# Rank scatter: 14 of 128 tiles as direct row copies, five scatters split into 2 and 126 rows

## The chip, the cores and the metric

One core of a Trainium2 chip. The metric is the device time of one execution in microseconds; lower is better. The core has a matrix engine (PE), a vector engine (DVE), GpSimd (POOL), ScalarE (ACT), SyncE (SP), and 16 DMA engines that all transfers share. SP and ACT issue plain transfers, POOL issues the indirect ones.

## The reference

Eight batches of 2048 rows, each row 2560 floats (10,240 bytes). Each row goes to the place that its score has among the 2048 scores of its batch.

```python
B, N, D = 8, 2048, 2560           # x: (B, N, D), scores: (B, N)
order = np.argsort(scores, axis=1)
ranks = np.argsort(order, axis=1)
out = np.zeros_like(x)
out[np.arange(B)[:, None], ranks, :] = x
```

x and out have 167.8 MB each; a rank is the number of scores in the batch that are smaller (plus the equal ones that stand earlier).

## The kernel before

The rows are cut into 128 tiles (b, t) of 128 rows: eight batches b, sixteen tiles t in each. All waits are placed by hand: each engine has a counter (`Line`), and `after` makes one engine wait for another's count.

- **Ranks.** The scores (64 KB) are loaded once, turned on PE into `s_col` (a score per partition), and for each batch spread over all partitions into `s_all` (PE into `ps_all`, DVE copies it, L206). For each tile DVE then counts with three reductions (L225) how many scores are smaller, adds the three counts (L248, L254) into `rank`, and turns it into whole numbers in `rank_i` (L265). DVE works through the tiles in order and never waits for the rows.
- **Loads.** `load` (L294) brings tile k of 128 rows, 1.28 MB of `x`, into buffer k % 16. The loads alternate between SP (even k) and ACT (odd k). The first sixteen go out at once; a later one first waits (`scatter_done`) until the scatter of the tile that had its buffer, sixteen before, has landed.
- **Scatters.** POOL goes through the tiles in order (`scatter`, L345). For each it waits for the load and for DVE's ranks, and issues an indirect DMA that writes the 128 rows of the buffer to the 128 rows of `out` that `rank_i` names.
- **The lists.** `DIRECT[b]` names the tiles of batch b that are not loaded and scattered but copied by rows, and `SPLIT` the tiles whose scatter is issued in two pieces: the last `LAST` = 2 rows with their own copy of the ranks (`rank_t`, on the first partitions), and the other 126. `BULK` is the list of the tiles that are loaded, `ROWS` of those that are copied. In the kernel before, both lists are empty, so all 128 tiles are in `BULK` and the code for rows and pieces makes no instructions.
- **Order on SP and ACT.** The lists of the two queues are written out in one loop over k, from NBUF = 16 on: ahead of load k all groups of rows come that are due by then, alternately on SP and ACT:

```python
for k in range(NBUF, NB):
    while n < len(chunks) * (k - NBUF + 6) // (NB - NBUF + 6 + 6):
        rows(*two[n % 2], *chunks[n])
        n += 1
    load(two[k % 2][0], k)
```

A group (`chunks`) has G = 16 rows, so a tile copied by rows has eight groups.

Of the kernel before, what the change touches and what calls it, by code (L numbers as in the profile page):

```python
# [40 lines left out]
def kernel(  # L41
# [7 lines left out]
    B, N, D = x.shape  # L49
# [3 lines left out]
    T = N // P  # L53


    DIRECT = [()] * B

    SPLIT = ()
    LAST = 2
    ORDER = [list(range(T)) for b in range(B)]  # L60
    BULK = [(b, t) for b in range(B) for t in ORDER[b] if t not in DIRECT[b]]
    ROWS = [(b, t) for b in range(B) for t in DIRECT[b]]
    NB = len(BULK)
# [28 lines left out]
    with tc.tile_critical(no_gpsimd_drain=True):  # L92
# [86 lines left out]
        def from_psum():  # L179
            b, t, tick = pending  # L180
            dve.after(pe, tick)
            col = b * T + t
            if t in DIRECT[b]:
                t_rows[b, t] = dve.did(
# [16 lines left out]
        for b in range(B):  # L201
# [12 lines left out]
            for t in ORDER[b]:  # L214
# [43 lines left out]
                if pending is not None:  # L258
                    from_psum()
                    pending = None  # L260
                direct = t in DIRECT[b]
                if not direct:
# [4 lines left out]
                if direct:  # L267
# [5 lines left out]
                    ))  # L273
                elif (b, t) in SPLIT:
                    pe.after(dve, dve.n)
# [22 lines left out]
        def scatter_done(line, k):  # L298
            line.wait(s_scat[k % NBUF], 16 * (k // NBUF + 1))
            n = sum(1 for j in range(k % NBUF, k + 1, NBUF) if BULK[j] in SPLIT)  # L300
            if n:
# [40 lines left out]
        def scatter(k, lo, hi, index, sem):  # L342
            b, t = BULK[k]
            col = b * T + t
            nc.gpsimd.indirect_dma_start(  # L345
                out=out_flat,
                out_offset=bass.IndirectOffsetOnAxis(
                    ap=index[:hi - lo, col:col + 1], axis=0
                ),
                in_=xb[k % NBUF][lo:hi, :],  # L350
                in_offset=None,
                element_offset=b * N * D,
            ).then_inc(sem, 16)

        for k, (b, t) in enumerate(BULK):
            i = k % NBUF
            pl.wait(s_load[i], 16 * (k // NBUF + 1))
            pl.after(dve, t_bulk[b, t])
            if (b, t) in SPLIT:
                scatter(k, P - LAST, P, rank_t, s_last[i])  # L360
# [33 lines left out]
```

## Time and profile before

| | |
|---|---|
| median of 3 runs | 798.27 us (798.03 to 798.38) |
| profiled execution | 798.03 us |
| its span in the profile | 796.3 us |
| instructions in the profile | 1925 |
| busy: PE, DVE, POOL | 29.3, 422.3, 122.6 us |
| read from and written to HBM | 167.84 MB and 167.77 MB |
| 128 scatters: issue on POOL, median from issue to landing | 949 ns each, 87.4 us |
| 64 loads on SP: median from issue to landing | 10.3 us |

The span is cut into 40 equal slices in the profile, each digit the busy share of a slice in tenths. For the DMA engines the digit is the mean over the 16, and a line of GB/s says what they moved; a transfer is counted once, whether it goes in or out. A queue's share is the time that its packets took, as a share of 16 engines over the span. In a wait, "SPq" is SP's queue of DMA issues; behind the arrow stands what it waited for, then the time in all, how often, and the longest. In a table by windows each line has the window, its length, the busy time of PE, PE's weight loads, DVE and POOL with the number of instructions, the granted PE clock, the DMA share and the GB/s. In the timeline a line has the start and the time from the first to the last of the instructions merged in it, which "x6" counts.

### The profile page before, as it was taken

To read this page: it belongs to the slowest core of one execution; us is meant where nothing else is said; L and a number is where in the kernel's file an instruction comes from. 1 tells how busy PE (TensorE), PEld (TensorE's weight loads), DVE (VectorE), ACT (ScalarE), POOL (GpSimd) and SP (SyncE) were. 2 spreads that over 40 slices of the span, in tenths; PEclk is the share of its full clock that TensorE was granted. 3 is DMA by queue.
4 is the path that set the end of the run, shared out by engine and by line. 5 is a ranking of instruction groups with operands and counts; after the bars stand their busy time and mean duration, and the time that the engine had idled before them with its cause. 6 is when DMAs were issued, how large, how long until landed. Compare 5 with 4: busy or idle time off the path is not lost.

```text
span 796.3 us, 1925 instructions
## 1 busy us (share of the span) xinstructions
PE 29.3 (4%) x144; PEld 26.4 (3%) x144; DVE 422.3 (53%) x1170; POOL 122.6 (15%) x136
## 2 busy tenths in 40 slices
PE   3001001010010010010000000000000000000000
PEld 3001001010010010010000000000000000000000
DVE  6999999999999999999999200000000000000000
POOL 1211121111111111111111111111111111111100
PEclk9555555555555555555555555555555555555555
DMA  9999999999999999999999999999999999999995
GB/s 360 423 429 427 428 429 429 428 429 427 429 427 429 428 430 429 430 428 428 428 428 428 430 430 430 428 429 429 428 428 430 430 430 429 428 429 428 428 430 219
DMA packets 36893, 335.74 MB, mean 422 GB/s; under 512 B 4104, under 2 KB 4104, under 8 KB 4104
## 3 DMA queue, kind: packets, MB, share of 16 engines
q0 software_dynamic: 18432, 167.78, 49.7%
q10 hardware_dynamic: 9216, 83.89, 24.9%
q1 hardware_dynamic: 9232, 83.96, 24.9%
q14 instruction: 12, 0.10, 0.0%
q8 instruction: 1, 0.02, 0.0%
HBM read 167.84 MB, written 167.77 MB: 421 GB/s over the span
## 4 chain that ended last, share of the span: by engine, by line
another core or an unknown queue 81%; DMA 7%; DVE 3%; ACTq 2%; PE 1%; issue 0%; POOL 0%; SPq 0%; POOLq 0%
DMA out_dram<-x,rank_i 6%; ACTq L294 2%; DVE trash L225 2%; DMA x<-in_x_dram 1%; PE ps_all L161 0%; DMA s_in<-in_scores_dram 0%; PE ps_col L140 0%; DVE rank L254 0%; DVE rank L248 0%; POOL out_dram L345 0%; DVE rank_i L265 0%; DVE s_all L206 0%; DVE s_col L148 0%; SPq L389 0%
## 5 line engine op out<-in xcount | busy, mean ns | idle before, releaser
L225 DVE TENSOR_SCALAR_CACHE_REDUCE trash<-s_all,s_col 128x256 bf16<-128x256 f32 (+15 forms) x248 | 315.1, 1307 | 0.3
L345 POOL DMA_INDIRECT out_dram<-x,rank_i x128 | 121.5, 949 | 626.7 <-DMA x<-in_x_dram 435.6
L225 DVE SCALAR_TENSOR_TENSOR trash<-s_all,s_col,mask 128x128 bf16<-128x128 f32 x128 | 44.5, 347 | 0.0
L161 PE MATMUL ps_all<-ident,s_col 128*128 128x128 f32 x128 | 27.4, 403 | 307.8 <-DVE s_all L206 307.4
L161 PEld LDWEIGHTS ps_all<-ident,s_col 128*128 128x128 f32 x128 | 24.6, 215 | 310.3 <-DVE s_all L206 309.8
L254 DVE TENSOR_TENSOR rank<-rank,acc 128x1 f32<-128x1 f32 x128 | 20.5, 160 | 4.4
L248 DVE TENSOR_TENSOR rank<-acc,acc 128x1 f32<-128x1 f32 x128 | 20.4, 159 | 4.4
L265 DVE CAST rank_i<-rank 128x1 int32<-128x1 f32 x128 | 19.7, 154 | 4.5
L206 DVE COPY s_all<-ps_all 128x512 f32<-128x512 f32 x32 | 20.2, 684 | 2.2 <-PE ps_all L161 1.6
L225 DVE DVE_READ_ACCUMULATOR trash<-s_all,s_col 128x1 f32 x248 | 20.5, 83 | 0.0
L225 DVE DVE_READ_ACCUMULATOR trash<-s_all,s_col,mask 128x1 f32 x128 | 10.5, 82 | 0.0
L148 DVE COPY s_col<-ps_col 128x128 f32<-128x128 f32 x1 | 0.3, 292 | 4.6 <-PE ps_col L140 4.6
L140 PE MATMUL ps_col<-ident,s_in 8*128 8x8 f32 x16 | 1.9, 250 | 4.0 <-DMA s_in<-in_scores_dram 4.0
L140 PEld LDWEIGHTS ps_col<-ident,s_in 8*128 8x128 f32 x16 | 1.8, 216 | 4.0 <-DMA s_in<-in_scores_dram 4.0
L135 DVE MEMSET acc<- 128x128 f32 x1 | 0.2, 165 | 1.1 <-SPq L92 1.1
L111 POOL TENSOR_SCALAR_AFFINE_SELECT ident<-ident 128x128 f32<-128x128 f32 x1 | 0.3, 283 | 0.1
L123 POOL TENSOR_SCALAR_AFFINE_SELECT mask<-mask 128x128 f32<-128x128 f32 x1 | 0.3, 283 | 0.0
L107 POOL MEMSET ident<- 128x128 f32 x1 | 0.2, 204 | 0.5 <-SPq L92 0.5
L108 POOL MEMSET mask<- 128x128 f32 x1 | 0.2, 202 | 0.0
L378 POOL MEMSET const-float32-0.0<- 128x1 f32 x1 | 0.1, 99 | 0.3 <-issue 0.3
L378 POOL MEMSET const-uint8-127<- 128x1 uint8 x1 | 0.1, 120 | 0.0
L378 POOL MEMSET const-bfloat16-1.0<- 128x1 bf16 x1 | 0.1, 114 | 0.0
(1 smaller groups left out, 0.1 us busy)
## 6 DMA issues: line engine op xcount, KB each, us to landing
x<-in_x_dram ACTq DMA_DIRECT2D x64, 1280.0 KB
x<-in_x_dram SPq DMA_DIRECT2D x64, 1280.0 KB, 10.3
out_dram<-x,rank_i POOLq DMA_INDIRECT x128, 87.4
s_in<-in_scores_dram SPq DMA_DIRECT2D x1, 64.0 KB
```

The costliest lines, as they stand in the source:

```text
L111: nc.gpsimd.affine_select(out=ident[:], in_=ident[:], pattern=[[-1, P]], compare_op=OP.not_equal, fill=1.0, base=0, channel_multiplier=1,)
L123: nc.gpsimd.affine_select(out=mask[:], in_=mask[:], pattern=[[-1, P]], compare_op=OP.is_ge, fill=0.0, base=-1, channel_multiplier=1,)
L140: nc.tensor.transpose(out=ps_col[:, B * c:B * (c + 1)], in_=s_in[:, P * c:P * (c + 1)], identity=ident[:B, :B],)
L161: nc.tensor.transpose(out=ps_all[:, P * c:P * (c + 1)], in_=s_col[:, c, b:b + 1].to_broadcast([P, P]), identity=ident[:],)
L206: nc.vector.tensor_copy(out=s_all[:, 512 * q:512 * (q + 1)], in_=ps_all[:, 512 * q:512 * (q + 1)],)
L225: how.pop("do")(out=trash[i][:, :P * (hi_t - lo_t)], in0=s_all[:, P * lo_t:P * hi_t], accum_out=acc[which][:, cols], **how,)
L248: nc.vector.tensor_tensor(out=rank[:, cols], in0=acc[0][:, cols], in1=acc[1][:, cols], op=OP.add)
L254: nc.vector.tensor_tensor(out=rank[:, cols], in0=rank[:, cols], in1=acc[2][:, cols], op=OP.add)
L265: nc.vector.tensor_copy(out=rank_i[:, cols], in_=rank[:, cols])
L294: line.eng.dma_start(out=xb[i][:], in_=x[b, P * t:P * (t + 1), :]).then_inc(s_load[i], 16)
L345: nc.gpsimd.indirect_dma_start(out=out_flat, out_offset=bass.IndirectOffsetOnAxis(ap=index[:hi - lo, col:col + 1], axis=0), in_=xb[k % NBU ...
L378: nc = _bacc.Bacc("TRN2", target_bir_lowering=False, num_devices=1)
```

## The change

```diff
-    DIRECT = [()] * B
-
-    SPLIT = ()
+    DIRECT = [(4, 5)] * 6 + [(4,)] * 2
+
+    SPLIT = [(b, 8) for b in range(2, 7)]
```

- **Rows.** Tiles 4 and 5 of batches 0 to 5 and tile 4 of batches 6 and 7, fourteen tiles of 1792 rows, leave `BULK`, which has 114 tiles then. For each of them PE turns the ranks into one row (`ps_row`, L270), and DVE makes byte offsets of them (`rows_i`, L185) in place of the cast at L265, after the two additions of the next tile. Each of the 112 groups waits for that tile's offsets, loads 16 of them into registers of SP or ACT (L306), and issues 16 DMAs (L316). Each of these copies one row of 10,240 bytes from `x` to `out`, without a buffer; in the built program it is an access of 16 pieces of 640 bytes.
- **Their place.** With NB = 114 six groups stand ahead of load 16, three on each queue; from there on about one group comes with each load, and eight groups, four on each queue, follow after the last load. At the end SP and ACT also wait for all rows.
- **Pieces.** The scatter of tile 8 in batches 2 to 6 becomes two indirect DMAs on POOL, rows 126 and 127 first, then rows 0 to 125. PE picks out the two ranks (L277) and DVE copies them to `rank_t` (L196) after the additions of the next tile. A load into that buffer waits for both.
- The counting on DVE, the sixteen buffers and the order of the other tiles stay as they are. POOL has 119 indirect DMAs in place of 128, SP 954 DMAs in place of 65, ACT 953 in place of 64.

## The prediction

> **What bounds the kernel now.** I read the page first: the forty slices, then the DMA queues.
>
> ```profile
> PE   3001001010010010010000000000000000000000
> ...
> DVE  6999999999999999999999200000000000000000
> POOL 1211121111111111111111111111111111111100
> ...
> DMA  9999999999999999999999999999999999999995
> GB/s 360 423 429 427 428 429 429 428 429 427 429 427 429 428 430 429 430 428 428 428 428 428 430 430 430 428 429 429 428 428 430 430 430 429 428 429 428 428 430 219
> ```
>
> The 16 DMA engines are busy from the first slice to the last but one at a constant 429 GB/s; DVE, which counts the ranks, is done past the middle and POOL is nearly idle. The rate does not change when DVE stops, so DVE does not set it.
>
> ```profile
> DMA packets 36893, 335.74 MB, mean 422 GB/s; under 512 B 4104, under 2 KB 4104, under 8 KB 4104
> ...
> q0 software_dynamic: 18432, 167.78, 49.7%
> q10 hardware_dynamic: 9216, 83.89, 24.9%
> q1 hardware_dynamic: 9232, 83.96, 24.9%
> q14 instruction: 12, 0.10, 0.0%
> ```
>
> Each tile passes the engines twice: as a load (q1 for SP, q10 for ACT) and as a scatter (q0). The three shares add to 99.5%. All small packets are semaphore increments. Then the waits of the queues, and of the scatters:
>
> ```profile
> SPq L294 <- DMA out_dram<-x,rank_i: 708.0, 56, 24.3
> ```
> ```profile
> POOL out_dram L345 <- DMA x<-in_x_dram: 435.6, 84, 7.0
> ```
>
> SP waits 708 us for scatters to free buffers; POOL waits mostly for loads. The ring load, scatter, buffer is held up by the engines alone, with some fourteen scatters in backlog (87.4 us from issue to landing, at 6.1 us a tile). Last the end, by windows:
>
> ```profile
> 100.00:780.00 680.00, 18.27 (x80) 16.38 (x80) 332.54 (x926) 102.30 (x108) 0.51 1.01 429
> ...
> 785.00:786.00 1.00, 0.00 (x0) 0.00 (x0) 0.00 (x0) 0.00 (x0) 0.50 0.87 369
> 786.00:787.00 1.00, 0.00 (x0) 0.00 (x0) 0.00 (x0) 0.00 (x0) 0.50 0.22 92
> 787.00:789.00 2.00, 0.00 (x0) 0.00 (x0) 0.00 (x0) 0.00 (x0) 0.50 0.12 51
> 789.00:792.40 3.40, 0.00 (x0) 0.00 (x0) 0.00 (x0) 0.00 (x0) 0.50 0.06 24
> 792.40:796.30 3.90, 0.00 (x0) 0.00 (x0) 0.00 (x0) 0.00 (x0) 0.50 0.01 2
> ```
>
> 429 GB/s over 16 is 26.8 GB/s an engine. So most engines end at 786.0 us, and from 789 to 792.4 the 24 GB/s are one engine alone, 6.4 us late. After that 3.9 us of ending follow.
>
> **The price of a row now.** A 10,240-byte row takes 10240/26.8 = 382 ns of one engine per pass, its share of semaphore packets included. A tile is 8 load rows and 8 scatter rows per engine, 16 x 0.382 = 6.11 us, which the spacing of SP's loads confirms (12.2 us for two tiles). Per row of a tile: 6.11/128 = 47.7 ns of every engine.
>
> **The change, part by part.** *Fourteen tiles as row copies.* 1,792 rows go from x to out directly. Each is one DMA of 16 pieces of 640 bytes, one piece and one semaphore increment per engine. Each byte passes the engines once, not twice, but in small pieces. The trace has no 640-byte packet and no copy between two DRAM tensors. From below: 640/10240 x 382 = 24 ns of data, plus 6 ns for the increment (in the packet records of the tail, 387 ns from row to row with an increment between and 381 without), 30 ns. From above: an increment or 32-byte packet lasts 7 to 9 ns, nearly all fixed cost; 24 + 7 + 9 = 40 ns. Farther above: each byte billed for its reading and for its writing, as in a load and a store, 2 x 24 + 7 + 9 = 64 ns. The far ends: a first packet of the scores' load, with nothing pipelined ahead, took 773 ns on average for 8 KB against 307 ns in a full pipe; I leave those 466 ns out because other queues keep the pipe full here. I take 24 + 7 + 6 = 37 ns, near the additive bound, as fixed costs are what the small packets show. Gain per row 47.7 - 37 = 10.7 ns; times 1,792, 19.2 us off every engine. Without fixed cost it is 31.7 us; at 47.7 ns nothing.
>
> The Trainium skill speaks against taking the pure byte price: "DMA: Bandwidth & Descriptors", section "How a descriptor splits into AXI transactions", lets a piece that starts off a 256-byte boundary fetch wasted beats, so of 640-byte pieces every second one takes 24 beats for 20; with the 3 beats per packet of "Why small descriptors are slow" and 1.2 ns a beat (385 ns for 320) I estimate 33 ns with the increment on one half of the engines, 38 on the other, and the dearer half would make the gain 17 us. No run here shows it yet.
>
> *Issuing them.* SP and ACT each gain 896 row DMAs and 56 register loads, ahead of and between their loads. The price of an issue:
>
> ```profile
> 2.34 3.54 SPq L294 DMA_DIRECT2D x<-in_x_dram  x6
> ```
> ```profile
> 30.22 0.33 SPq L294 DMA_DIRECT2D x<-in_x_dram  x1
> ```
>
> 0.33 us alone, 0.59 us when both queues issue back to back. I take 0.59, as both will issue in runs of 16. A register load of 16 offsets has no row; bounds are nothing and a few issues (2 us); I take 1 us. One load and one group of 16 rows on a queue: 0.33 + 1 + 16 x 0.59 = 10.8 us. The engines need, for the two queues' two tiles and 32 rows, 2 x 6.11 + 32 x 0.037 = 13.4 us. So issue hides under the engines, with 2.6 us spare; it stops hiding at (13.4 - 1.33)/16 = 0.75 us a row.
>
> *What stands behind the rows.* The 17th and 18th loads, the first on each queue to reuse a buffer, now wait behind three groups each. Their offsets exist when DVE has finished tile 5, near 30 us, so the 17th load goes from 30.2 us to about 30 + 3 x 10.4 = 61 us. By then POOL will have issued some eleven scatters (one per 3.2 us from 14.8, less the two row tiles): with 16 loads 27 passes, 27 x 3.05 = 82 us of engine work. The engines don't run dry; the cover is 21 us and is gone at 1.0 us a row. Later a freed buffer waits up to one group, about 10 us of the backlog's 87. Four groups per queue come after the last load: 42 us against 53 us that now pass from ACT's last load at 738.9 to the last scatter's landing. Hidden.
>
> *Split scatters.* Five tiles go as 2 and 126 rows: five more POOL starts, against fourteen fewer; at 0.95 us each and 627 us of POOL idle, nothing. On DVE fourteen casts (154 ns) go, nineteen small copies out of PSUM come, the nearest 292 ns: about 3 us more, beside a DVE that has ended 340 us early. The scatters that wait for them (on tile 8 of batches 2 to 6) are by then late for loads. PE's 19 small operations lie in 308 us of idle. On the engines: 126 rows do not divide by 16. If 14 engines carry 9 rows each, they pay one row more per split, 5 x 0.382 = 1.9 us; the engines of the 2 rows carry one instead of eight and save 5 x 7 x 0.382 = 13.4 us. An even deal would cost 0. I take 1.9. (The Trainium skill, same page, section "Why a DMA increments its semaphore by 16 and not by 1", says that the largest divisor up to 16 is used, 14 for 126; the scores' load of 8 rows left 16 packets above 9,216, 8 data and 8 increments, which agrees.)
>
> *The late engine.* 6.4 us may be the instruction fetches (q14), if one engine does them; some 2,000 more instructions at 12 packets of about 0.33 us per 1,925 add 4 us. If the splits relieve this very engine (10.4 - 13.4 - 1.9 is below zero) it is no longer last; if they miss it, it is 10.4 us late. The trace doesn't say which; between the ends I take 3.2 us, nearer to relief.
>
> **Sum.** Engines 786.0 - 19.2 + 1.9 = 768.7; late engine 3.2; ending 3.9: a span of 775.8 us. The profiled execution took 798.03 us at a span of 796.3, 1.7 more, and lies 0.24 below the median; so 777.5, which I round to 777.
>
> **Rivals.**
> *Issue-bound (slower).* Rows with a register address issue slower than the 0.59 us seen for loads, or a row's ring turn behind 382 ns packets of the other queues sets the pace. The queue then lasts 30 + 56 x (16t + 1) + 57 x 0.33: past 768.7 from t = 0.74 us. At 0.85 it is 867 us, and 872 with the ending. For it: 0.82 us is the longest SP load issue at the start. Against: alone it is 0.33. Chance 0.12.
> *Copies between DRAM tensors cost both sides (slower).* At 64 ns a row the engines gain 29 us: 786.0 + 29.2 + 1.9 + 3.2 + 3.9 + 1.7 = 826. It is slower from about 50 ns, where 1,792 x 2.3 eats what the late engine gives. Against: a load and a scatter both cost 382 ns a row, so the end of the transfer hasn't mattered. Chance 0.07.
> *Dear but under break-even:* 42 to 48 ns or a late engine missed, 790 to 796. Chance 0.08.
> *Cheap:* 30 ns and a relieved engine: 786.0 - 31.7 + 0 + 3.9 + 1.7 = 760. Chance 0.08.
> *The sides cancel,* within 0.2% (1.6 us, about what a measurement of this kernel can tell from no change): 0.03.
> *Forecast,* 761 to 790: 0.62.
>
> **The numbers.** The range 761 to 796 holds the forecast, the dear case, half of the cheap and the cancelled one: about 0.77; widening it to the slower rivals at 826 and 872 would cover a gap that no case fills. Faster 0.62 + 0.08 + 0.08 = 0.78; same 0.03; slower 0.19.
>
> **What would show it.** Bytes fall by 14 x 1.31 = 18 MB to about 317, with 28,672 packets of 640 bytes and as many more increments. The engines' share stays at nine tenths in all slices and the rate falls to about 410 GB/s. SP still waits hundreds of us for scatters. The tail below full rate shrinks from 6.4 us. Slices below nine tenths, an SP that waits for no scatter, or rows issued at 0.75 us or more would prove the issue rival; full engines with a longer span, the second.

## The result and the profile after

The changed kernel takes 948.93 us (median of 4, 948.25 to 951.51) against 798.33 us: 1.189 times as long, 95% interval 1.187 to 1.192. The forecast was 777 us with a range to 796. The side was wrong: of the rivals, "issue-bound (slower)" was the right one in kind, with 872 us at the row price of 0.85 us that it took as its example.

The page of the changed kernel, the slices and the DMA queues:

```profile
span 946.5 us, 5641 instructions
...
DMA  9999999999999999899998899899999989999841
GB/s 367 424 427 416 357 382 359 343 374 335 365 327 371 329 371 322 297 353 319 381 302 308 313 341 365 313 337 342 350 344 327 319 307 377 350 359 360 314 162 20
DMA packets 90474, 317.74 MB, mean 336 GB/s; under 512 B 32568, under 2 KB 61240, under 8 KB 61240
...
q0 software_dynamic: 16656, 149.43, 39.2%
q10 hardware_dynamic: 36880, 83.95, 28.6%
q1 hardware_dynamic: 36896, 84.01, 25.5%
q14 instruction: 41, 0.34, 0.1%
```

The bytes fall to 317.74 MB as forecast. The rate was to fall to about 410 GB/s. It is 416 to 427 in slices 2 to 4, until 95 us, and from slice 5 on it swings between 297 and 382, until the list of rows runs out in the last two. The digits stay at 8 or 9 until then: the records count time in which a packet moves less than it could (between 100 and 870 us a 10,240-byte packet on ACT's queue takes 497 ns on average, against 385 in the kernel before), so a busy share near one with fewer bytes than 429 GB/s is no proof of work. Who waits for whom, SP first, then POOL:

```profile
SPq L306 <- DVE trash L225: 26.4, 2, 25.5
...
SPq L92 <- DMA out_dram<-in_x_dram: 6.3, 1, 6.3
```
```profile
POOL out_dram L345 <- DMA x<-in_x_dram: 652.0, 46, 40.5
```

SP waited 708 us for scatters before, and doesn't wait for one now. That and slices below nine tenths are two of the signs that the prediction had named for the issue rival. Buffers are free; the loads come late, and POOL waits 652 us for them, up to 40.5 us at a time. The timeline of SP's queue in the middle shows why: one load, sixteen rows, one load, without a pause.

```profile
427.88 14.16 SPq L316 DMA_DIRECT2D out_dram<-in_x_dram  x16
442.10 0.71 SPq L294 DMA_DIRECT2D x<-in_x_dram  x1
443.92 13.42 SPq L316 DMA_DIRECT2D out_dram<-in_x_dram  x16
457.39 1.17 SPq L294 DMA_DIRECT2D x<-in_x_dram  x1
459.68 14.67 SPq L316 DMA_DIRECT2D out_dram<-in_x_dram  x16
474.44 0.59 SPq L294 DMA_DIRECT2D x<-in_x_dram  x1
```

Load to load is 16 us, where the sum had 10.8 for the list and 13.4 for the engines. By line and operation (durations least, median, greatest):

```profile
L316 SPq DMA_DIRECT2D out_dram<-in_x_dram x896: 3/557/3152, 31.6 to 931.2; - x180
```
```profile
L306 SPq TENSOR_LOAD <-rows_i x56: 967/1159/2937, 29.9 to 920.3; - x56
```

The median row is issued in 557 ns, near the 0.59 us assumed, but the tail reaches 3.2 us. Added up over SP's records, from each start to the next: rows 725.6 us (0.81 each, the third sign), moves of their addresses 58.6, register loads 79.0, loads 66.9, of which 25 are the first wait for ranks. These 930 us are nearly all of the span. The list of SP, and ACT's like it, is the bound. Why a row whose issue needs 0.56 us takes 0.81 is what the experiments had to find.

### The profile page after: what moved, and what is told of

Its sections match the earlier page's. It is cut to its first block, busy times and chain, and to the rows that moved or that the text cites. A ratio compares the mean times of both kernels' runs of the same rounds, so it can differ in the third digit from the quotient of the medians.

```text
span 946.5 us, 5641 instructions
## 1 busy us (share of the span) xinstructions
PE 35.0 (4%) x168; PEld 27.7 (3%) x168; DVE 422.1 (45%) x1175; POOL 114.3 (12%) x127
## 2 busy tenths in 40 slices
DMA packets 90474, 317.74 MB, mean 336 GB/s; under 512 B 32568, under 2 KB 61240, under 8 KB 61240
## 3 DMA queue, kind: packets, MB, share of 16 engines
q10 hardware_dynamic: 36880, 83.95, 28.6%
## 4 chain that ended last, share of the span: by engine, by line
issue 48%; DVE 43%; POOL 5%; PE 1%; DMA 0%; POOLq 0%; SPq 0%
DVE trash L225 35%; POOL out_dram L345 5%; DVE rank L248 2%; DVE rank L254 2%; DVE s_all L206 2%; DVE rank_i L265 2%; PE ps_all L161 0%; DMA s_in<-in_scores_dram 0%; DVE rows_i L185 0%; PE ps_col L140 0%; POOLq L28 0%; DVE s_col L148 0%; DVE rank_t L196 0%; SPq L389 0%; SPq L92 0%
## 5 line engine op out<-in xcount | busy, mean ns | idle before, releaser
L345 POOL DMA_INDIRECT out_dram<-x,rank_i x114 | 108.8, 955 | 740.4 <-DMA x<-in_x_dram 596.4
L265 DVE CAST rank_i<-rank 128x1 int32<-128x1 f32 x114 | 17.3, 152 | 3.5
L345 POOL DMA_INDIRECT out_dram<-x,rank_t x5 | 4.3, 865 | 56.0 <-DMA x<-in_x_dram 55.7
L270 PE MATMUL ps_row<-ident,rank 128*1 128x128 f32 x14 | 5.2, 372 | 147.2 <-DVE rank L254 117.6
L225 DVE DVE_READ_ACCUMULATOR trash<-s_all,s_col,mask 128x1 f32 x128 | 10.3, 81 | 0.0
L270 PEld LDWEIGHTS ps_row<-ident,rank 128*1 128x1 f32 x14 | 1.1, 79 | 151.3 <-DVE rank L254 119.5
L185 DVE TENSOR_SCALAR rows_i<-ps_row 1x128 int32<-1x128 f32 x14 | 3.8, 272 | 0.0
L277 PE MATMUL ps_last<-rank,ident 128*2 128x1 f32 x10 | 1.0, 164 | 50.3 <-DVE rank_i L265 50.3
L277 PEld LDWEIGHTS ps_last<-rank,ident 128*2 128x2 f32 x10 | 0.4, 82 | 51.8 <-DVE rank_i L265 51.8
L196 DVE CAST rank_t<-ps_last 2x1 int32<-2x1 f32 x5 | 0.7, 139 | 0.0
## 6 DMA issues: line engine op xcount, KB each, us to landing
out_dram<-x,rank_i POOLq DMA_INDIRECT x114, 14.8
```

What stands on the lines that cost most here:

```text
L185: nc.vector.tensor_scalar(out=rows_i[ROWS.index((b, t))][:], in0=ps_row[:1, :P], scalar1=float(b * N), scalar2=float(ROW), op0=OP.add, op1 ...
L196: nc.vector.tensor_copy(out=rank_t[:, col:col + 1], in_=ps_last[:LAST, col:col + 1])
L225: how.pop("do")(out=trash[i][:, :P * (hi_t - lo_t)], in0=s_all[:, P * lo_t:P * hi_t], accum_out=acc[which][:, cols], **how,)
L265: nc.vector.tensor_copy(out=rank_i[:, cols], in_=rank[:, cols])
L270: nc.tensor.transpose(out=ps_row[:1, :P], in_=rank[:, cols], identity=ident[:])
L277: nc.tensor.matmul(out=ps_last[:LAST, cols], lhsT=ident[:, P - LAST:], rhs=rank[:, cols], start=True, stop=True,)
```

## The experiments

Each ratio is against runs of the kernel before on the same chip, with its 95% interval. Unless said otherwise `SPLIT = ()`.

**First, parts of the change.** Rows without splits:

```diff
-    SPLIT = [(b, 8) for b in range(2, 7)]
+    SPLIT = ()
```


> The fourteen row tiles, no split scatters. Issue theory (the lists of SP and ACT are the bound: about 30 us, then 56 groups of 16 rows at 0.875 us a row and 1.4 us for the register load, then the loads): 949 us, unchanged within 0.5%, since POOL and the late DMA engine are not on the path. If the split scatters cost the time (126 rows on few engines): much faster, below 850 us.

942.86 us, ratio 1.181 (1.179 to 1.183), a little below the 949 us within 0.5%. The rows alone make the loss; the splits add 6 us to it.

Splits without rows:

```diff
-    DIRECT = [(4, 5)] * 6 + [(4,)] * 2
+    DIRECT = [()] * B
```


> No row tiles, five scatters split. If a split relieves the engine that ends 6.4 us late before: 798.3 - 6.4 + 1.9 = about 794 us. If it relieves other engines: 798.3 + 1.9 = about 800 us. If 126 rows fall on one engine: over 900 us.

808.36 us (803.8 to 813.5), ratio 1.014 (1.011 to 1.017). Worse than either way of relief on the list and far from the 900 us, so none of the three cases, and with more spread than most kernels here. From 790 to 796 us its windows still show 97 to 148 GB/s, the work of four to six engines after the others have ended, where before it was one.

Half the rows:

```diff
-    DIRECT = [(4, 5)] * 6 + [(4,)] * 2
+    DIRECT = [(4,)] * 7 + [()]
```


> Seven row tiles (896 rows), no splits: half the row DMAs. Issue theory: a queue's list lasts about 30 + 28 x 15.4 + 60 x 0.65 = 500 us, under the engines' time, so the engines bind again and the bytes saved show: 798.3 - 896 x (47.7 - 39 ns) = about 790 us, with SP waiting for scatters again for over 200 us. Engine theory (small packets slow the DMA engines themselves): half of the loss stays, about 873 us.

814.66 us, ratio 1.020 (1.019 to 1.022). Neither: far from half the loss, and still a loss. The issue of a row had grown, not shrunk. SP's timeline here:

```profile
496.34 28.58 SPq L316 DMA_DIRECT2D out_dram<-in_x_dram  x16
524.97 0.57 SPq L294 DMA_DIRECT2D x<-in_x_dram  x1
```

28.6 us for sixteen rows, 1.8 us each. The price of an issue isn't fixed: with fewer rows the DMA engines were busier (402 GB/s on average against 336) and the queue waited more for them. The median landing of SP's loads is 49.0 us, from 10.3 before: loads stand behind rows within the queue too.

Fewer bytes in each row:

```diff
-                    out=out_bytes[bass.ds(at[i], ROW)],
-                    in_=x_bytes[b, P * t + G * q + i, :],
+                    out=out_bytes[bass.ds(at[i], 1024)],
+                    in_=x_bytes[b, P * t + G * q + i, :1024],
```
(with the splits of the changed kernel)


> As the changed kernel, but each row DMA copies only the first 1,024 of the 10,240 bytes (16 pieces of 64 bytes); the rest of those rows is left out. Issue theory with a price of its own per DMA: 949 us within 3%. If the issue waits for the engines to take the bytes, or the engines are the bound: the engines lose 1,792 x 21 ns = 38 us of work each, and the time falls by 30 us or more, to 910 us or less.

The kernel leaves out nine tenths of each copied row. Four runs, 916 to 942 us: the spread is nearly as wide as the difference asked about, and the lowest lies between the two expectations. Against 949 us the bytes left out are worth 7 to 33 us of the 150; the runs say no more.

**Second, the price on the engines against the place in the queues.** My reading of the seven tiles was that a row costs the engines 66 ns, not 37. Two row tiles:

```diff
+    DIRECT = [(4,)] * 2 + [()] * 6
```


> Two row tiles (256 rows, in batches 0 and 1), no splits: so few that neither list of SP or ACT is near its limit. Dear-copy theory (from seven tiles: (814.66 - 798.46)/896 = 18 ns a row lost net, so 66 ns of every engine): 798.5 + 256 x 18 ns = 803 us. The 37 ns on record: 798.5 - 256 x 10.7 ns = 796 us. Pure issue theory (the copies are cheap, the lists are the bound): also 796 us.

796.42 us, ratio 0.9973 (0.9963 to 0.9983): a gain. (798.49 - 796.42)/256 = 8 ns a row, against 10.7 in the prediction. The 66 ns fell.

Rows on ACT alone and loads on SP alone, seven tiles:

```diff
-            rows(*two[n % 2], *chunks[n])
+            rows(*two[1], *chunks[n])
...
-            load(two[k % 2][0], k)
+            load(two[0][0], k)
```


> Seven row tiles, all their rows on ACT, all loads on SP. Dear-copy theory: as with both queues, about 815 us, since the engines have the same packets. Order theory (loads come late because they stand behind rows in a list): the loads are free of that, the engines fill and the time falls under 800 us. If one list alone issues at 0.9 us a row or more: 30 + 896 x 0.9 = 836 us or more, and ACT ends last.

1005.57 us, ratio 1.260 (1.258 to 1.262): of the expectations the last, ACT ends last. But its windows hold the answer to the other two:

```profile
100.00:740.00 640.00, 20.07 (x85) 16.77 (x85) 331.59 (x922) 96.34 (x101) 0.51 1.02 426
760.00:1000.00 240.00, 0.00 (x0) 0.00 (x0) 0.00 (x0) 0.00 (x0) 0.50 0.12 21
```

Until 740 us the engines run at 426 GB/s with rows among the packets: loads that don't share a queue with rows keep them full. All loads and scatters end as early as in a good kernel, and 240 us of rows follow. ACT's timeline while the other queues are at work, and after:

```profile
399.11 25.92 ACTq L316 DMA_DIRECT2D out_dram<-in_x_dram  x18
```
```profile
800.00 25.03 ACTq L316 DMA_DIRECT2D out_dram<-in_x_dram  x36
```

1.4 us a row beside loads and scatters, 0.7 us alone (register loads included). So one row waits for the others. In the trace's packet records an engine serves 32 packets of the loads and 32 of the scatters in 25 us, and 36 of the 18 rows (a piece and an increment each). With the increments of loads and scatters counted too, it is 37 packets of each of the three queues in 25.92 us: one packet of each queue in turn. The order shows it as well. From one start to the next a row packet holds its engine for 381 ns, a piece for 28 and an increment for 6; with these times the packets between 200 and 300 us can be followed along each engine, not without a slip here and there, and they go scatter, load, piece, scatter, load, increment, and so on: after a packet of the rows comes one of the scatters in 2,085 cases of 2,297, and after a scatter one of the loads in 2,254 of 2,287. So a row needs two turns, and each turn lasts two packets of 382 ns. The first seventy rows or so go out unhindered. From 200 to 700 us the rows that are issued and not yet begun stay between 32 and 35: the queue holds that many, and then issuing waits for room.

Two runs tried what in a row costs the engines:

```diff
-                    out=out_bytes[bass.ds(at[i], ROW)],
-                    in_=x_bytes[b, P * t + G * q + i, :],
+                    out=out_bytes[bass.ds(at[i], ROW)].rearrange("(e p n) -> e p n", e=16, p=2),
+                    in_=x_bytes[b, P * t + 16 * q:P * t + 16 * q + 16, :1280].rearrange("e (p n) -> e p n", p=2)[:, :, :320],
```


> Seven row tiles, each row DMA as 32 pieces of 320 bytes, two for each engine, with one increment as before; for this the source is other bytes of x, so those rows' content is not the reference's. If the fixed price of a row on an engine is the piece's (some 25 ns or more): 815 + 896 x 25 ns = 837 us or more. If it is the increment's: within 5 us of 815.

839.95 us, ratio 1.052 (1.051 to 1.054): the first case by its number. But each piece more is a turn more as well, so this run can't tell a dearer row from a longer wait.

```diff
+    fixed = pool.tile([16, ROW // 4 // 16], F32, name="fixed_row")
...
+        t_fixed = pl.did(nc.gpsimd.memset(fixed[:], 0.0))
...
+            line.after(pl, t_fixed)
...
-                    out=out_bytes[bass.ds(at[i], ROW)],
-                    in_=x_bytes[b, P * t + G * q + i, :],
+                    out=out_bytes[bass.ds(at[i], ROW)].rearrange("(e n) -> e n", e=16),
+                    in_=fixed[:].bitcast(U8),
```


> Seven row tiles, each row written from one fixed SBUF tile of zeros (16 partitions of 640 bytes) and not read from x; the content of those rows is left out. If copying between two DRAM tensors is what costs (a small read from HBM that the engine waits for): down by 10 us or more, under 805 us. If it is the number of small packets: within 5 us of 815.

836.72 us, ratio 1.050 (1.047 to 1.053). Neither; reading from SBUF is no relief (SP's 448 rows take 613 us from start to start, 610 with x as the source), so the copy between two DRAM tensors isn't what costs. Why it is 22 us slower than with x stays open; its register loads took 2.6 us each, against 1.4.

**Third, the turn theory made to predict.** Few enough rows that ACT ends in time:

```diff
+    DIRECT = [(4,)] * 4 + [()] * 4
...
+            rows(*two[1], *chunks[n])
...
+            load(two[0][0], k)
```


> Four row tiles (512 rows), all rows on ACT, all loads on SP. Turn theory (while scatters and loads both keep the engines full, ACT gets a row out every 1.40 us): 30 + 512 x 1.40 = 747 us, under the engines' time, so the full gain shows: 798.5 - 512 x (47.7 - 37.5 ns) = 793 us, the fastest so far. If the price of a row on the engines is 66 ns after all: 808 us.

792.85 us, ratio 0.993 (0.992 to 0.994), where 793 was expected: faster than both kernels, and the fastest of all that ran. Its control, without rows:

> No row tiles, no splits; only the loads move, all on SP. Both theories: 798.5 us within 0.3%, since the engines are full either way. If one queue is worth something by itself, the runs with rows on ACT have to be read against this one.

798.51 us, ratio 1.000 (0.999 to 1.001). So the gain is the rows': (798.51 - 792.85)/512 = 11.1 ns each, which makes 47.7 - 11.1 = 36.6 ns the price of a row on the engines, give or take 2 to 3 ns by the intervals of the two ratios. The 28 and 6 ns from start to start in the packet records add to 34.

The same rows with rows and loads alternating on both queues:

> Four row tiles with rows and loads alternating on both queues, as in the changed kernel. Engine price alone: 798.5 - 512 x 10.2 ns = 793 us. Turn theory: each group of 16 rows is 32 packets on its queue, ahead of loads of 9, so loads land later with each group; between two tiles (796.4) and seven (814.7), nearer to two as the scatters in backlog still cover it: 795 to 800 us, and a median landing of SP's loads between 10 and 49 us.

798.63 us, ratio 1.000 (0.999 to 1.001), as expected, and SP's loads land after 46.6 us. The gain of 5.7 us is lost by the place of rows and loads in the queues alone.

Then the test of the turns: seven tiles on ACT as in the run of 1005.57 us, but each load in two DMAs of half the columns, so that its packet is half as long.

```diff
-            line.eng.dma_start(
-                out=xb[i][:], in_=x[b, P * t:P * (t + 1), :]
-            ).then_inc(s_load[i], 16)
+            for h in range(2):
+                line.eng.dma_start(
+                    out=xb[i][:, D // 2 * h:D // 2 * (h + 1)],
+                    in_=x[b, P * t:P * (t + 1), D // 2 * h:D // 2 * (h + 1)],
+                ).then_inc(s_load[i], 16)
...
-            pl.wait(s_load[i], 16 * (k // NBUF + 1))
+            pl.wait(s_load[i], 32 * (k // NBUF + 1))
```


> Seven row tiles, rows on ACT and loads on SP, but each load as two DMAs of half the columns, so that a load's packet is 5,120 bytes. Turn theory (a row's piece and its increment each wait for one packet of every other queue): twice as many turns pass for the same loads, a row takes at most 30 / (2 x 1.9) = 0.8 us, the list of ACT lasts 30 + 896 x 0.8 = 750 us, and the time falls from 1005.6 us to about 800. If the price of issuing is ACT's own, or hangs on the bytes in flight: 1005 us within 3%.

795.30 us, ratio 0.996 (0.995 to 0.997): 210 us less for an edit that touches no row. All 896 rows are unhindered now; first the run with whole loads, then this one:

```profile
L316 ACTq DMA_DIRECT2D out_dram<-in_x_dram x896: 524/556/1834, 32.9 to 1000.4; - x180
```
```profile
L318 ACTq DMA_DIRECT2D out_dram<-in_x_dram x896: 524/550/953, 31.7 to 746.2; - x180
```

The greatest is 953 ns, where it was 1,834, and the last row is issued at 746 us, not at 1000.

**Fourth, the same for the fourteen tiles.** The loads past the sixteenth move to POOL, each issued after a scatter and eight tiles ahead, with semaphores of their own; SP and ACT issue the rows as in the changed kernel.

```diff
+    AHEAD = 8
...
-            load(two[k % 2][0], k)
+            pass
...
             scatter(k, 0, P, rank_i, s_scat[i])
+            if NBUF <= k + AHEAD < NB:
+                load(pl, k + AHEAD)
```


> All fourteen row tiles, no splits; SP and ACT issue the first sixteen loads and then rows alone, and POOL issues the other loads, each after a scatter and eight tiles ahead. Turn theory: a row's two packets wait for one big packet each, 2 x (0.382 + 2 x 0.03) = 0.88 us at most, near the 0.81 us that issuing with its register loads takes unhindered, so each list lasts 30 + 896 x 0.81 to 0.88 = 756 to 820 us, and the time is the larger of that and 798.5 - 1,792 x 10.2 ns = 780: 780 to 825 us. If 0.875 us a row is the price of a row DMA with fourteen tiles whatever stands beside it, and the loads' place means nothing: over 900 us.

798.92 us, ratio 1.001 (1.000 to 1.002), within the 780 to 825, with all 1,792 rows: 144 us less than the same rows beside loads. The control:

> No row tiles, no splits; loads past the sixteenth on POOL as in rows14_pool_loads. If POOL's queue with loads and scatters keeps the engines full: 798.5 us within 1%. What it differs by is the price of that order, to be taken off the run with rows.

802.99 us, ratio 1.006 (1.004 to 1.007). SP's rows in rows14_pool_loads and the rate:

```profile
L318 SPq DMA_DIRECT2D out_dram<-in_x_dram x896: 517/546/2203, 32.4 to 771.6; - x180
```
```profile
100.00:720.00 620.00, 21.66 (x90) 17.05 (x90) 333.06 (x928) 136.05 (x177) 0.51 1.03 417
740.00:760.00 20.00, 0.00 (x0) 0.00 (x0) 0.00 (x0) 2.39 (x3) 0.50 0.85 332
```

The engines keep 417 GB/s, near the 410 of the forecast, until they run out of loads before 760 us. From start to start SP's rows take 574.9 us in all, against 748.1 in rows14_whole: 173 us of waiting for turns are gone, more than the 144 that the time falls. The list still ends late, at 772 us, so I took two tiles off:

```diff
+    DIRECT = [(4, 5)] * 4 + [(4,)] * 4
```


> As rows14_pool_loads with twelve row tiles (1,536 rows). Turn theory: each list lasts about 60 + 48 x (16 x 0.705 + 2.0) = 697 us, well under the engines' time, so the control of 803.0 less the bytes saved shows: 803.0 - 1,536 x 10.2 ns = 787 us, the fastest of all. If rows cost more in larger numbers whatever stands beside them: 795 us or more.

798.48 us, ratio 1.000 (0.999 to 1.001). Missed by 11 us, and not through the rate. The end by windows:

```profile
760.00:774.00 14.00, 0.00 (x0) 0.00 (x0) 0.00 (x0) 1.90 (x2) 0.50 0.54 228
774.00:790.00 16.00, 0.00 (x0) 0.00 (x0) 0.00 (x0) 0.00 (x0) 0.50 0.06 27
```

27 GB/s is one engine. Fifteen have ended by 774 us, near what was computed, and one goes on alone for 16 us (6.4 before). The instruction fetches on q14 have grown from 12 packets to 37; at 0.33 us each that is 8 us, if this engine has them all. The rest isn't explained. It is so in rows14_pool_loads too: 27 GB/s, one engine alone, from 774 to 790 us. The 799 us of that run are set by this engine and not by the rows; the other fifteen end where the forecast of 780 us would have them.

**Last, the splits.** An even deal over the sixteen engines:

```diff
-    LAST = 2
+    LAST = 16
```
(no row tiles, splits as in the changed kernel)


> No row tiles; the same five scatters split into 16 and 112 rows, both even over 16 engines. If the 10 us of the split into 2 and 126 come from the uneven deal: 798.5 us within 0.3%. If they come from the added waits, POOL starts or semaphores: 805 to 810 us again.

819.11 us (814 to 823), ratio 1.027 (1.025 to 1.029): neither case, and worse than 2 and 126. The deal isn't the cause. The packet records, followed as above, show it for the first split of each run: 16 and 112 rows come as one and then seven on each of the 14 engines that can be followed through, evenly; of 2 and 126 rows twelve engines carry nine of the 126, as the prediction assumed, which costs 1.9 us for five splits and not 10. And the splits added to rows12_pool_loads, whose one late engine they might relieve:

> rows12_pool_loads with the five splits into 2 and 126 rows of the changed kernel. If the pieces of 2 rows take rows off the engine that ends late (5 x 7 x 0.382 = 13.4 us at most): 798.5 - 13 = 785 us or a little more. If they fall on other engines: 798.5 + 2 us or more, with the late engine still alone at the end.

802.55 us, ratio 1.004 (1.003 to 1.005), with 24 GB/s, one engine, still alone from 784 us. The second case: the late engine is not relieved. What makes the engines end apart when scatters are split stays open.

## Why the prediction was wrong, step by step

**What bounds the kernel before** was right: the engines, by bytes and packets. loads_one_queue moves half the loads to another queue and changes nothing.

**The price of a row on the engines**, 37 ns against 47.7, was right: 36.6 ns by rows4_one_queue and its control. The far end of 64 ns, a row billed on both sides, is excluded where the queues are full. The estimate from the Trainium skill had 33 and 38 ns for the two halves of the engines; the 36.6 ns alone could not tell it apart, but the packet records show no such halves: between 100 and 700 us of rows7_one_queue 6,865 of 6,890 pieces last 32 ns.

**The step that failed is "Issuing them".** It priced a group on a queue at 10.8 us, from issues of loads, and compared this with the engines' 13.4. Measured are 16 us. Of its terms, the issue itself was right (557 ns median; 0.65 us from row to row when nothing hinders it, with the move of the address, 65 ns, that the sum did not have), and the register load was 1.4 us on SP and 1.7 on ACT for 1 assumed. With these, 16 x 0.65 + 1.4 + 0.7 = 12.5 us, still under 13.4. What was missing is a term: the issue waits when the queue is full, and a row leaves the queue in two turns of the engines. The issues of the kernel before that I priced from could not show the full queue: the loads at the start went into empty ones. I named the mechanism in one clause of the rival ("a row's ring turn behind 382 ns packets"), and did not work it out: two turns of two packets, 2 x 2 x 0.382 = 1.5 us, twice the 0.75 at which the forecast turns, was computable. The row price was there, and so was the premise: between 20 and 60 us, while all three queues of the kernel before have work, the packets of an engine go scatter, SP's load, ACT's load in turn, and an increment has a turn of its own. The rival should have had far more than 0.12.

**How 1.5 us become 0.81** in the changed kernel: the turns don't stay that long. Loads late behind rows empty the backlog of scatters; their median landing falls from 87.4 to 14.8 us:

```profile
out_dram<-x,rank_i POOLq DMA_INDIRECT x114, 14.8
```

So turns get shorter and the engines get less to do, at some 340 GB/s. Why it settles at just this rate is argued, not derived. That the waiting on rows, not their number or their copies, is the 150 us is shown by rows14_pool_loads: same rows, same issuing, hardly any waiting (0.64 us a row from start to start, 0.83 in rows14_whole), 799 us.

**What stands behind the rows** counted the cover of the backlog once, at the start, and the cover held there: the rate is 416 to 427 GB/s from 24 to 95 us. The step did not ask how fast the backlog is made up again.

**The splits** were priced at 1.9 us and measured 10 alone, 6 with the rows, 4 with POOL's loads. **The late engine** was taken as half relieved; no run with splits shows it relieved. Both are small here.

The Trainium skill's "DMA: Bandwidth & Descriptors" has the rule in "Queues, rings and completion order": an engine goes round between the queues that have work, a whole packet at a time. The runs here agree on the round. Of the size they show something else than the page's typical 9 to 17 descriptors: a turn is one row of 10,240 bytes, one piece or one increment, 37 of each queue in 25.92 us. Its section "Issuing engines are not separate DMA queues" says that issuing from several engines saves only the sequencers' time, as all run on the same 16 DMA engines. For equal packets that agrees (798.51 us with all loads on one queue). For small packets beside large ones it leaves out something: rows4_whole and rows4_one_queue have the same DMAs on two queues and differ by 5.8 us by which queue has what.

## What to carry to other kernels

Before putting many small DMAs beside large ones, count turns, not only bytes: packets per small DMA, times the other queues at work, times their packet's length, and compare it with the time that you have for each. Keep small DMAs in a queue without bulk loads behind them (four tiles gained by it; seven lost 207 us, as ACT's list became the bound), and if they come out too slowly, shorten the packets of the others: halving the loads' packets took 210 us off one kernel here. An issue that was cheap into an empty queue says nothing about one into a full queue, and a DMA share of 0.97 at 342 GB/s, as here between 100 and 870 us, is a sign of waiting, not of work.

## What the hardware showed that I had not expected

- The issue of one row DMA takes 0.55 us alone and 1.47 us beside two full queues, with no wait named in the profile: the time is inside the instruction.
- With seven row tiles on both queues an issue is slower (1.4 us from start to start) than with fourteen (0.81): the price follows what the other queues do.
- Splitting five of 128 scatters, with no byte more, costs 10 us without rows, and 21 when both pieces are dealt evenly over the 16 engines.
- One DMA engine ends 6.4 us after the others in the kernel before and 16 us or more in rows12_pool_loads and rows14_pool_loads.
- A DMA engine goes round the queues one packet at a time, and an increment of 4 bytes has a turn like a row of 10,240.
